# The first layer's modulation vectors summed on TensorE in column strips instead of on three other engines

## The chip, the cores and the metric

The kernel runs on one core of one Trainium2 chip. A core has TensorE (PE; its weight loads are shown as PEld), VectorE (DVE), ScalarE (ACT), GpSimd (POOL), SyncE (SP, whose queue issues nearly all transfers) and 16 DMA engines. The metric is the device time of one execution in microseconds. A time of the kernel is the median of several executions; the profile is one further execution with its own time.

## The reference

Two blocks run one after the other on a sequence of 256 rows and 1024 features, all in fp32. The first block has two layers. Each layer begins with a modulation vector of 6 x 1024 numbers (shift, scale and gate for the mixer, the same three for the feed-forward), made from one conditioning vector:

```python
c_act = jax.nn.silu(c)                       # [1, 1024]
for l in range(DEPTH):                       # DEPTH = 2
    mod = c_act @ w_mod[l] + b_mod[l]        # [1, 6144]
    shift1, scale1, gate1, shift2, scale2, gate2 = split(mod, 6)
    h = rms_norm(x, norm1) * (1.0 + scale1) + shift1
    proj = h @ w_in                          # pooled part, q, keys and values, gates
    ...                                      # pooling mixer, sparse attention
    x = x + gate1 * (mix @ w_out)
    h2 = rms_norm(x, norm2) * (1.0 + scale2) + shift2
    x = x + gate2 * (square(relu(h2 @ w_ff1)) @ w_ff2)
```

The second block (a state-space branch, a dilated attention, a feed-forward) has no modulation. What matters here is `c_act @ w_mod[l]`: a vector of 1024 times a matrix of 1024 x 1024 for each of the six parts.

## The kernel before

Large products run on TensorE as three products of rounded fp32 halves (high and low). Every weight tile of 128 x 1024 lands in one of five staging slots (`wst`); ScalarE makes the high half and VectorE the low one (`wh` L139, `wl` L140), and then the slot is free. Matrix products accumulate in four PSUM banks (`acc`); two banks (`st`), one (`tr`) and one (`pv`) serve everything else: scores, transposes, small products.

A modulation part is a sum over 1024 rows of the matrix, each scaled by one activation. The kernel keeps the activations as a tile `cact` of 128 x 8, so a tile of 128 matrix rows is scaled by one column of it. There are two routines. `first_mod(c)` (L603 to L617) makes, for 256 features of shift and scale, eight scaled sums of 128 x 512: VectorE adds the even ones (L611, L614), ScalarE scales the odd ones (L612, L615) and GpSimd adds them (L616). `first_norm` then sums over the partitions with eight products with a matrix of ones (`tr<-cst,acc`), makes the columns `mcol` (L627, L629), scales the transposed normed input (L638) and splits it into `hh` and `hl`. This is done in four parts, one for each quarter of the features; the products of q and k for part c, 24 on TensorE, follow it in `start()`. The four parts are staggered: the sums of part c+1 are written behind the q weight of part c.

`mod_part(l, q, eng)` (L536 to L580) makes a whole part of 1024 numbers in steps, one 512 KB tile a step. With `eng` 3, as for the first layer's parts 2, 3 and 4 (the mixer's gate, the feed-forward's shift and scale), five of eight tiles are added by VectorE (L547), three are scaled by ScalarE (L549) and added by GpSimd (L550) into `macc`. A gate is then split (L558, L559) and summed over the partitions into all rows (`mgate`); a shift or scale becomes a column (`mcol`). The steps are not placed by hand: each load of a weight tile takes as many of them as `rate` says.

```python
            self.due += self.rate
            while self.due >= 1.0 and self.extra:
                self.due -= 1.0
                self.step()
```

The rate is 0 at first and becomes `r0b` = 2 at step 14 of the first layer's plan. Gates are asked for by the residual after the output projection, shift and scale of the feed-forward just behind it. Five wide buffers of 128 x 1024 (`t4`) hold `macc` and `mgate`. The attention's steps are placed among the products by a plan with due times; within these bounds a scheduler fixes each engine's order ahead of time.

Of the kernel before, what the change touches and what calls it, by code (L numbers as in the profile page):

```python
# [16 lines left out]
D = 1024  # L17
# [7 lines left out]
ALPHA = 2.0 ** 0.25  # L25

SZ = 1024
TU = dict(nst=5, tabc=2, nw=9, nt2=22, raw=1, krest=2, qrest=4, pool2=1, c2=3, c3=1, c4=1, ln=3, uv='uv', pre=[1], nv=5, nv1=0, nv0=0, u0=19.5, du=0.7, ub=2, uc=4, c0=32.5, dc=0.1, w0=36, dw=0.5, comp=22, pool=27, dpool=2, cmpa=32, cmpb=34, dcmp=2, e1=1, e0=1, pta=2, ahead=3, modp=3, rf=0.95, r0=0, r0b=2, r1=0.8, r1b=1.2, rs=14, raw_=4, qrest_=6, u0_=19.5, du_=1.0, comp_=22, pool_=26, cmpa_=31, cmpb_=35, nv_=0, nv0_=0, w0_=32, dw_=0.8, order2='v0 qk0 qk1 qk2 v1 B C x0 x1 z0 x2 z1 x3 z2 z3 g2 g3 pa g0 g1 ps', dts=8, dcd=30, par0=10, par1=40, d0=50, dd=2, db=3, dc2=5, ss0=73, ds=4.2, scb=5, sx=3, sr=6, sg=3.5, sy=3.5, sn=8, sf=300, mf0=5, modp1=99, rf1=0.5, pool2_=3, c3_=2, c4_=3, nv1_=2, dpool_=2, dcmp_=1, dc_=0.4, cap=4, ub_=2.5, c0_=32.5, pta_=4)
NST, NW = TU['nst'], TU['nw']
NT2, NT4, NS5 = TU['nt2'], 5, 20  # L30

# [30 lines left out]
def tile_two_blocks(ctx: ExitStack, tc: tile.TileContext, I, out, stop=None, dbg=None):  # L62
# [451 lines left out]
    V.reciprocal(cact, cact)  # L514
    V.tensor_tensor(cact, cact, csrc, op=OP.mult)

    parc = [small.tile([128, NPS], FT, name=f"parc{l}", bufs=1) for l in range(DEPTH)]
    par = {}

# [17 lines left out]
    def mod_part(l, q, eng):  # L537
# [14 lines left out]
        if q in (2, 5):  # L552
            gt = t4([128, D], "mgate")
            parts = []
            for n in range(2):
                ns = slice(n * 512, (n + 1) * 512)
                ah, al = t2([128, 512], "mah", FR), t2([128, 512], "mal", FR)
                A.activation(ah, acc[:, ns], AF.Copy)  # L558
                G.tensor_tensor(al, acc[:, ns], ah, op=OP.subtract)  # L559
                parts.append((ah, al))  # L560
            for _ in range(3):
                yield
            for n, (ah, al) in enumerate(parts):
                b = bank("tr")
                mm(b, ones_r, al, True)
                mm(b, ones_r, ah, False, True)
                A.activation(gt[:, n * 512:(n + 1) * 512], b, AF.Copy)
            MC[l, q] = gt
        else:
            for _ in range(2):  # L570
                yield
            b = bank("tr")
            for j in range(8):
                mm(b[:, j * 64:(j + 1) * 64], acc[:, j * 128:(j + 1) * 128], ones[:, 0:64], j == 0, True)
            c = small.tile([128, 8], FT, name="mcol", bufs=6)
            i = {0: 0, 1: 1, 3: 2, 4: 3}[q]
            V.tensor_tensor(c, b.rearrange("p (j n) -> p j n", j=8)[:, :, 0], PS(l, "bmod")[:, i * 8:i * 8 + 8], op=OP.add)
            if q in (1, 4):
                V.scalar_tensor_tensor(c, c, 1.0, PS(l, "norm1" if q == 1 else "norm2"), op0=OP.add, op1=OP.mult)
            MC[l, q] = c  # L580

    ones_r = cp.tile([128, 128], FR, name="ones_r")

# [16 lines left out]
        xn = rms(t)  # L600
        later(TU["ln"], lambda: to_fm(t, xn, hi, lo, MC[l, q0 + 1], MC[l, q0]))

    def first_mod(c):  # L603

        acc = [t2([128, 512], "acc0") for _ in range(2)]
        for j in range(4):
            st = wp.tile([128, SZ], FT, name="wst", bufs=NST)
            nc.sync.dma_start(st, I["w_mod0"][c, j])
            sv, k = [st[:, i * 512:(i + 1) * 512] for i in range(2)], 2 * j
            if j == 0:  # L610
                V.tensor_scalar(acc[0], sv[0], cact[:, k:k + 1], None, op0=OP.mult)  # L611
                A.activation(acc[1], sv[1], AF.Copy, scale=cact[:, k + 1:k + 2])  # L612
            else:
                V.scalar_tensor_tensor(acc[0], sv[0], cact[:, k:k + 1], acc[0], op0=OP.mult, op1=OP.add)  # L614
                A.activation(sv[1], sv[1], AF.Copy, scale=cact[:, k + 1:k + 2])  # L615
                G.tensor_tensor(acc[1], acc[1], sv[1], op=OP.add)  # L616
        return acc  # L617

    def first_norm(xn, acc, hi, lo, c):
# [5 lines left out]
        m = small.tile([128, 4], FT, name="mcol0", bufs=2)  # L625
        bm = PS(0, "bmod")[:, 0:16].rearrange("p (q k) -> p q k", q=2)
        V.tensor_tensor(m.rearrange("p (q k) -> p q k", q=2), b[:, :256].rearrange("p (q k n) -> p q k n", q=2, k=2)[:, :, :, 0],  # L627
                        bm[:, :, 2 * c:2 * c + 2], op=OP.add)
        V.scalar_tensor_tensor(m[:, 2:4], m[:, 2:4], 1.0, PS(0, "norm1")[:, 2 * c:2 * c + 2], op0=OP.add, op1=OP.mult)  # L629
        b = bank("pv")  # L630
        for k in range(2):
            f = 256 * c + 128 * k
            for t in range(2):
                T.transpose(b[:, k * 256 + t * 128:k * 256 + t * 128 + 128], xn[t][f // 512][:, f % 512:f % 512 + 128], ident)
        hf = t2([128, 512], "hf")
        for k in range(2):
            ks = slice(k * 256, (k + 1) * 256)
            V.tensor_scalar(hf[:, ks], b[:, ks], m[:, 2 + k:3 + k], m[:, k:k + 1], op0=OP.mult, op1=OP.add)  # L638
        split(fl(hi[:, 2 * c:2 * c + 2]), fl(lo[:, 2 * c:2 * c + 2]), hf, A)

    def hybrid_layer(l, hilo, between, done):
# [1104 lines left out]
```

## Time and profile before

| what | value |
|---|---|
| time, median of 3 runs | 1291.28 us (1290.51 to 1297.46) |
| profiled execution, time | 1291.87 us |
| profiled execution, span from first to last instruction | 1290.1 us |
| TensorE busy | 1191.4 us, 92% |
| VectorE busy | 905.7 us, 70% |
| ScalarE busy | 640.3 us, 50% |
| GpSimd busy | 294.7 us, 23% |
| granted TensorE clock, mean | 0.973 |

Busy time is the time in which an engine ran an instruction. A busy TensorE need not be at its peak: its products are pipelined, and each row's duration has some drain in it that the next product overlaps. The first layer's q and k are made in about the first 65 us, its attention and output projection until about 180, its feed-forward until about 372.

### The profile page before, as it was taken

What the parts mean: (1) busy time and instruction counts of PE and PEld (TensorE: products, weight loads), DVE (VectorE), ACT (ScalarE), POOL (GpSimd) and SP (SyncE); (2) the same over time, 40 slices, a digit from 0 to 9 for tenths busy, and PEclk for the clock granted to TensorE, in tenths of its full rate; (3) what the DMA queues carried; (4) which work ended last, traced back from release to release, by engine and by line L of the source; (5) the groups of instructions that cost most, each with busy time, mean ns of one, the idle gap of its engine ahead of it and who ended that gap; (6) DMA issues with size and microseconds to landing.
All of it is one profiled execution on the core that took longest, in us unless ns stands there. A gap on an engine that the chain in (4) does not pass through costs nothing.

```text
span 1290.1 us, 19186 instructions
## 1 busy us (share of the span) xinstructions
PE 1191.4 (92%) x7242; PEld 1047.4 (81%) x7242; DVE 905.7 (70%) x1384; ACT 640.3 (50%) x1068; POOL 294.7 (23%) x281
## 2 busy tenths in 40 slices
PE   4868898999988999999999999998989999999997
PEld 3656776898977788799998999787688998789896
DVE  5877898877858768754446467899997557754544
ACT  4436355435436555645444355665674434554540
POOL 3543313103224101201010001434553001210101
PEclk9888989999999999999999999989998999999999
DMA  7855767998867525665654455244354643666640
GB/s 267 304 158 174 242 197 242 313 328 292 310 208 248 172 83 165 196 211 179 195 173 150 156 174 166 66 131 119 111 181 131 196 147 99 215 214 191 183 144 33
DMA packets 97028, 240.73 MB, mean 187 GB/s; under 512 B 9252, under 2 KB 14372, under 8 KB 96936
## 3 DMA queue, kind: packets, MB, share of 16 engines
q1 hardware_dynamic: 96296, 238.73, 57.8%
q8 instruction: 57, 0.93, 0.3%
q10 hardware_dynamic: 640, 0.79, 0.2%
q14 instruction: 35, 0.29, 0.1%
HBM read 237.65 MB, written 1.05 MB: 185 GB/s over the span
## 4 chain that ended last, share of the span: by engine, by line
PE 38%; issue 10%; DVE 9%; ACT 1%; POOL 1%; DMA 0%; DVEq 0%; ACTq 0%; POOLq 0%
PE acc L88 23%; PE st L88 12%; DVE wl L140 3%; DVE G L1420 2%; DVE E L1431 1%; PE pv L88 1%; DVE cv L1315 1%; ACT wh L139 1%; DMA wst<-in_w_up_dram 0%; POOL yss L118 0%; DVE yg L1462 0%; DVE ytmp L1450 0%; DVE yg L1457 0%; POOL fr L379 0%; PE tr L88 0%
## 5 line engine op out<-in xcount | busy, mean ns | idle before, releaser
L140 DVE TENSOR_TENSOR wl<-wst,wh 128x1024 fp32r<-128x1024 f32 (+3 forms) x340 | 427.3, 1269 | 173.0 <-ACT wh L139 171.4
L139 ACT ACTIVATE wh<-wst 128x1024 fp32r<-128x1024 f32 (+3 forms) x340 | 351.7, 1048 | 311.3 <-PE acc L88 113.6
L88 PE MATMUL st<-hh,wh 128*128 128x256 f32 x576 | 163.0, 283 | 0.0
L88 PE MATMUL st<-hl,wh 128*128 128x256 f32 x576 | 163.0, 283 | 0.0
L88 PE MATMUL st<-hh,wl 128*128 128x256 f32 x576 | 163.0, 283 | 0.0
L88 PE MATMUL acc<-wh,frl 128*128 128x512 f32 x384 | 151.2, 394 | 2.3 <-DVE frl L380 2.1
L379 POOL TENSOR_TENSOR fr<-fr 128x512 f32<-128x512 f32 x48 | 63.5, 1323 | 382.4 <-ACT frh L378 376.0
L88 PE MATMUL acc<-wl,frh 128*128 128x512 f32 x384 | 149.8, 390 | 0.0
L88 PE MATMUL acc<-wh,frh 128*128 128x512 f32 x384 | 149.7, 390 | 0.0
L88 PE MATMUL acc<-hh,wl 128*128 128x256 f32 x416 | 122.5, 295 | 2.3 <-DVE wl L140 2.3
L88 PE MATMUL acc<-hl,wh 128*128 128x256 f32 x416 | 119.9, 288 | 0.0
L88 PE MATMUL acc<-hh,wh 128*128 128x256 f32 x416 | 119.8, 288 | 0.0
L88 PEld LDWEIGHTS st<-hl,wh 128*128 128x128 f32 x576 | 110.5, 192 | 0.7
L88 PEld LDWEIGHTS st<-hh,wl 128*128 128x128 f32 x576 | 110.5, 192 | 0.7
L88 PEld LDWEIGHTS st<-hh,wh 128*128 128x128 f32 x576 | 110.5, 192 | 0.0
L88 PE MATMUL acc<-wl,hh 128*128 128x512 f32 (+3 forms) x224 | 89.7, 401 | 15.2 <-DVE wl L140 15.2
L547 DVE SCALAR_TENSOR_TENSOR macc<-wst,cact,macc 128x1024 f32<-128x1024 f32 x70 | 92.3, 1318 | 7.0 <-DMA wst<-in_w_mod_dram 4.5
L88 PE MATMUL acc<-wh,hl 128*128 128x512 f32 (+3 forms) x224 | 88.3, 404 | 3.3 <-DVE hl L105 2.7
L88 PE MATMUL acc<-wh,hh 128*128 128x512 f32 (+3 forms) x224 | 90.2, 403 | 0.0
L88 PEld LDWEIGHTS acc<-wh,frl 128*128 128x128 f32 x384 | 72.1, 188 | 19.3 <-DVE frl L380 5.4
L88 PEld LDWEIGHTS acc<-hh,wl 128*128 128x128 f32 x416 | 81.6, 196 | 4.7 <-DVE wl L140 3.1
L88 PEld LDWEIGHTS acc<-wh,frh 128*128 128x128 f32 x384 | 72.1, 188 | 15.3
(326 smaller groups left out, 2365.6 us busy)
## 6 DMA issues: line engine op xcount, KB each, us to landing
wst<-in_w_ff_dram SPq DMA_DIRECT2D x128, 512.0 KB, 4.4
wst<-in_w_mod_dram SPq DMA_DIRECT2D x96, 512.0 KB, 4.5
wst<-in_w_in_dram SPq DMA_DIRECT2D x92, 512.0 KB, 4.7
wst<-in_w_up_dram SPq DMA_DIRECT2D x32, 512.0 KB, 4.5
wst<-in_w_down_dram SPq DMA_DIRECT2D x32, 512.0 KB, 4.4
wst<-in_w_out_dram SPq DMA_DIRECT2D x24, 512.0 KB, 4.5
wst<-in_w_proj_ssd_dram SPq DMA_DIRECT2D x16, 512.0 KB, 3.6
wst<-in_w_in_dram SPq DMA_DIRECT2D x8, 384.0 KB, 3.8
```

What stands on the lines that cost most here:

```text
L88: T.matmul(o, l, r, start=start, stop=stop, skip_group_check=True)
L139: A.activation(h[:, :kc * n], st[:, :kc * n], AF.Copy)
L140: V.tensor_tensor(l[:, :kc * n], st[:, :kc * n], h[:, :kc * n], op=OP.subtract)
L379: G.tensor_tensor(r, r, r, op=OP.mult)
L547: V.scalar_tensor_tensor(acc, st, cact[:, k:k + 1], acc, op0=OP.mult, op1=OP.add)
L1315: V.scalar_tensor_tensor(v[:, a:e], u[:, a + j - 2:e + j - 2], w[:, j:j + 1], v[:, a:e], op0=OP.mult, op1=OP.add)
L1420: V.scalar_tensor_tensor(gm[:, i], cl, dt_[:, t, 32 + a0 + i:33 + a0 + i], gm[:, i], op0=OP.mult, op1=OP.add)
L1431: V.tensor_tensor(E, E, ssd.pop(("G", g, t, sub)), op=OP.mult)
```

## The change

All of `first_mod` and, for the first layer's parts 2, 3 and 4, `mod_part` give way to sums on TensorE. The activations are copied into a tile `cb` in which each of the eight columns stands 32 times. A product with 32 such columns as its weights gives 32 equal rows of sums in 32 of the 128 output partitions. The eight products of a group go to four strips of 32 columns by turns, two to each strip, so that the bank holds four partial sums, each 32 times. ScalarE copies the bank out. A product with a selector (`sel`, one row of each strip) adds the four and turns the row into columns; for the gate the selector stands in all 128 columns (`sel_all`), with the gate's bias added as row 1.

In the start, parts 0 and 1 are summed ahead of the first column sums, and part c+2 behind the k products of part c. The new `mod_sums` takes two tiles of 128 x 4 x 256 a step from the wide buffers, no longer from the weights' staging slots, and has five steps in place of ten or eleven. The rate `r0b` goes from 2 to 1.2. The remaining parts (those of the second layer, and the first layer's last gate) stay with `mod_part`.

```diff
+    cb = cp.tile([128, 8, 32], FT, name="cb")
+    V.tensor_copy(cb, cact[:, :, None].to_broadcast([128, 8, 32]))
+    sel = cp.tile([128, 2], FT, name="sel")
+    sel_all = cp.tile([128, 128], FT, name="sel_all")
...
+    def mod_sums(l, q):
+        acc = t4([128, D], "mrow")
+        def load(i):
+            ts = [t4([128, 4, 256], "mst") for _ in range(2)]
+            for j in range(2):
+                c = q * D + i * 256
+                nc.sync.dma_start(ts[j], I["w_mod"][l, j * 512:(j + 1) * 512, c:c + 256].rearrange("(k p) n -> p k n", p=128))
+            return ts
+        ts = load(0)
+        for i in range(4):
+            yield
+            b = bank("tr")
+            for k in range(8):
+                r = slice((k % 4) * 32, (k % 4) * 32 + 32)
+                mm(b[r, :256], cb[:, k], ts[k // 4][:, k % 4], k < 4, k >= 4)
+            A.activation(acc[:, i * 256:(i + 1) * 256], b[:, :256], AF.Copy)
+            if i < 3:
+                ts = load(i + 1)
+        if q in (2, 5):
+            nc.sync.dma_start(acc[1:2, :], I["b_mod"][l:l + 1, q * D:(q + 1) * D])
+            gt = t4([128, D], "mgate")
+            yield
+            for n in range(2):
+                ns = slice(n * 512, (n + 1) * 512)
+                b = bank("tr")
+                mm(b, sel_all, acc[:, ns], True, True)
+                A.activation(gt[:, ns], b, AF.Copy)
+            MC[l, q] = gt
+        else:
+            yield
+            b = bank("tr")
+            for j in range(8):
+                mm(b[:, 2 * j:2 * j + 2], acc[:, j * 128:(j + 1) * 128], sel, j == 0, True)
+            mod_columns(l, q, b[:, :16].rearrange("p (j n) -> p j n", j=8)[:, :, 0])
...
-    def first_mod(c):
-        acc = [t2([128, 512], "acc0") for _ in range(2)]
+    def first_rows(c):
+        b = bank("st")
         for j in range(4):
             st = wp.tile([128, SZ], FT, name="wst", bufs=NST)
             nc.sync.dma_start(st, I["w_mod0"][c, j])
-            sv, k = [st[:, i * 512:(i + 1) * 512] for i in range(2)], 2 * j
-            if j == 0:
-                V.tensor_scalar(acc[0], sv[0], cact[:, k:k + 1], None, op0=OP.mult)
-                A.activation(acc[1], sv[1], AF.Copy, scale=cact[:, k + 1:k + 2])
-            else:
-                V.scalar_tensor_tensor(acc[0], sv[0], cact[:, k:k + 1], acc[0], op0=OP.mult, op1=OP.add)
-                A.activation(sv[1], sv[1], AF.Copy, scale=cact[:, k + 1:k + 2])
-                G.tensor_tensor(acc[1], acc[1], sv[1], op=OP.add)
-        return acc
+            for i in range(2):
+                k = 2 * j + i
+                r = slice((k % 4) * 32, (k % 4) * 32 + 32)
+                mm(b[r], cb[:, k], st[:, i * 512:(i + 1) * 512], k < 4, k >= 4)
+        rows = t2([128, 512], "rows0")
+        A.activation(rows, b, AF.Copy)
+        return rows
...
-        for i in range(2):
-            for j in range(4):
-                mm(b[:, j * 64:(j + 1) * 64], acc[i][:, j * 128:(j + 1) * 128], ones[:, 0:64], i == 0 and j == 0, i == 1)
+        for j in range(4):
+            mm(b[:, 2 * j:2 * j + 2], rows[:, j * 128:(j + 1) * 128], sel, j == 0, True)
...
             accs = {n: [bank("acc") for _ in range(2)] for n in "qk"}
-            acc = first_mod(0)
-            first_norm(xn0, acc, hi, lo, 0)
+            rows = [first_rows(0), first_rows(1)]
+            first_norm(xn0, rows[0], hi, lo, 0)
             for c in range(4):
                 for n in "qk":
                     wh, wl = W.next()
-                    if n == "q" and c < 3:
-                        acc = first_mod(c + 1)
...
                     if n == "q" and c < 3:
-                        first_norm(xn0, acc, hi, lo, c + 1)
+                        first_norm(xn0, rows[c + 1], hi, lo, c + 1)
+                    if n == "k" and c < 2:
+                        rows.append(first_rows(c + 2))
...
+    for i in range(2):
+        V.reduce_sum(sel[:, i:i + 1], ident[:, 0:128:32], axis=AX.X)
+    V.tensor_tensor(sel_all, sel[:, 0:1].to_broadcast([128, 128]), ident[:, 1:2].to_broadcast([128, 128]), op=OP.add)
...
-    W.extra.extend(mod_part(*m, TU["modp"]) for m in MODS["mix", 0])
+    W.extra.extend(mod_sums(*m) for m in MODS["mix", 0])
```

## Rows read from the trace of the kernel before

**Rows 1.** The page's busy time, share of the span and instructions of each engine.
```profile
PE 1191.4 (92%) x7242; PEld 1047.4 (81%) x7242; DVE 905.7 (70%) x1384; ACT 640.3 (50%) x1068; POOL 294.7 (23%) x281
```
**Rows 2.** Busy time by stretch: us, engines with instructions, granted clock, DMA share, GB/s.
```profile
21.90:62.20 40.30, 33.53 (x142) 25.52 (x143) 32.16 (x38) 17.21 (x24) 20.29 (x21) 0.92 0.83 286
62.20:97.00 34.80, 24.27 (x110) 19.67 (x109) 25.86 (x57) 12.77 (x21) 17.07 (x31) 0.85 0.54 174
97.00:137.00 40.00, 29.70 (x176) 23.53 (x175) 28.83 (x72) 24.91 (x56) 14.52 (x14) 0.91 0.59 197
137.00:180.00 43.00, 42.15 (x265) 36.13 (x263) 38.90 (x91) 20.30 (x53) 13.06 (x6) 0.96 0.69 226
...
220.00:372.00 152.00, 149.31 (x953) 135.13 (x952) 116.08 (x105) 73.08 (x87) 35.49 (x29) 1.00 0.87 297
```
**Rows 3.** Waits of TensorE from 62 to 180: us in total, times, longest.
```profile
PE acc L88 <- DVE wl L140: 10.1, 3, 6.7
PE tr L88 <- DVE chv L836: 4.3, 1, 4.3
PE acc L88 <- DVE ml L105: 2.9, 1, 2.9
```
**Rows 4.** Groups by line, 0 to 62: count, busy us, mean ns, idle before.
```profile
L616 POOL TENSOR_TENSOR acc<-acc,wst 128x512 f32<-128x512 f32 x12 | 18.6, 1551 | 23.1 <-ACT wst L615 16.6 <-ACT acc L612 6.0
L614 DVE SCALAR_TENSOR_TENSOR acc<-wst,cact,acc 128x512 f32<-128x512 f32 x12 | 15.3, 1275 | 0.4
```
**Rows 5.** Groups by line, 62 to 180.
```profile
L550 POOL TENSOR_TENSOR macc<-macc,wst 128x1024 f32<-128x1024 f32 x9 | 21.3, 2369 | 42.5 <-DVE macc L547 26.4 <-ACT wst L549 16.1
L547 DVE SCALAR_TENSOR_TENSOR macc<-wst,cact,macc 128x1024 f32<-128x1024 f32 x15 | 19.1, 1275 | 2.2 <-POOL macc L550 2.2
```
**Rows 6.** Order of time in the start: start us, duration us, instruction, idle before.
```profile
8.89 0.72 ACT L612 ACTIVATE acc<-wst,cact 128x512 f32<-128x512 f32 x1
...
12.69 0.72 ACT L615 ACTIVATE wst<-wst,cact 128x512 f32<-128x512 f32 x1 [0.57 <-DMA wst<-in_w_mod_dram]
...
15.04 3.67 PE L88 MATMUL tr<-cst,acc 128*128 128x64 f32 x16 [3.50 <-DVE acc L614]
...
21.93 0.80 PE L88 MATMUL acc<-wh,hl 128*128 128x512 f32 x1 [0.56 <-DVE hl L105]
...
24.03 8.66 SPq L608 DMA_DIRECT2D wst<-in_w_mod_dram  x4
...
65.12 0.58 ACT L716 ACTIVATE kS<-acc 128x512 f32<-128x512 f32 x1
```
**Rows 7.** Order of time, single products on TensorE at several places.
```profile
22.53 0.63 PE L88 MATMUL acc<-wl,hh 128*128 128x512 f32 x1
...
97.51 1.13 PE L88 MATMUL st<-kT,qT 64*128 64x256 f32 x8
...
157.21 0.39 PE L88 MATMUL acc<-wh,ml 128*128 128x512 f32 x1
157.44 1.02 PE L88 MATMUL tr<-vbd,pcT 128*128 128x512 f32 x2
```
**Rows 8.** Order of time, places around waits from 55 to 136.
```profile
55.48 1.42 POOL L659 TENSOR_TENSOR tab<-par,cst 128x32 f32<-128x32 f32 x2 [3.93 <-DMA par<-in_par_dram]
...
68.12 1.66 POOL L118 TENSOR_TENSOR hr<-hss,half 128x8 f32<-128x8 f32 x1
...
81.49 2.37 POOL L550 TENSOR_TENSOR macc<-macc,wst 128x1024 f32<-128x1024 f32 x1
81.55 2.46 DVE L681 TENSOR_TENSOR sq<-sq,hr 128x128 f32<-128x128 f32 x1 [0.90 <-POOL hr L118]
...
113.81 1.18 DVE L678 TENSOR_TENSOR ckr<-ckr,csq 32x64 f32<-32x64 f32 x1
...
132.96 1.28 DVE L547 SCALAR_TENSOR_TENSOR macc<-wst,cact,macc 128x1024 f32<-128x1024 f32 x1 [0.71 <-POOL macc L550]
...
135.10 1.15 ACT L549 ACTIVATE wst<-wst,cact 128x1024 f32<-128x1024 f32 x1 [3.05 <-DMA wst<-in_w_mod_dram]
```

More of the change, by code (lines that the diff above doesn't have):

```diff
@@ L27 @@
 SZ = 1024
-TU = dict(nst=5, tabc=2, nw=9, nt2=22, raw=1, krest=2, qrest=4, pool2=1, c2=3, c3=1, c4=1, ln=3, uv='uv', pre=[1], nv=5, nv1=0, nv0=0, u0=19.5, du=0.7, ub=2, uc=4, c0=32.5, dc=0.1, w0=36, dw=0.5, comp=22, pool=27, dpool=2, cmpa=32, cmpb=34, dcmp=2, e1=1, e0=1, pta=2, ahead=3, modp=3, rf=0.95, r0=0, r0b=2, r1=0.8, r1b=1.2, rs=14, raw_=4, qrest_=6, u0_=19.5, du_=1.0, comp_=22, pool_=26, cmpa_=31, cmpb_=35, nv_=0, nv0_=0, w0_=32, dw_=0.8, order2='v0 qk0 qk1 qk2 v1 B C x0 x1 z0 x2 z1 x3 z2 z3 g2 g3 pa g0 g1 ps', dts=8, dcd=30, par0=10, par1=40, d0=50, dd=2, db=3, dc2=5, ss0=73, ds=4.2, scb=5, sx=3, sr=6, sg=3.5, sy=3.5, sn=8, sf=300, mf0=5, modp1=99, rf1=0.5, pool2_=3, c3_=2, c4_=3, nv1_=2, dpool_=2, dcmp_=1, dc_=0.4, cap=4, ub_=2.5, c0_=32.5, pta_=4)
+TU = dict(nst=5, tabc=2, nw=9, nt2=22, raw=1, krest=2, qrest=4, pool2=1, c2=3, c3=1, c4=1, ln=3, uv='uv', pre=[1], nv=5, nv1=0, nv0=0, u0=19.5, du=0.7, ub=2, uc=4, c0=32.5, dc=0.1, w0=36, dw=0.5, comp=22, pool=27, dpool=2, cmpa=32, cmpb=34, dcmp=2, e1=1, e0=1, pta=2, ahead=3, modp=3, rf=0.95, r0=0, r0b=1.2, r1=0.8, r1b=1.2, rs=14, raw_=4, qrest_=6, u0_=19.5, du_=1.0, comp_=22, pool_=26, cmpa_=31, cmpb_=35, nv_=0, nv0_=0, w0_=32, dw_=0.8, order2='v0 qk0 qk1 qk2 v1 B C x0 x1 z0 x2 z1 x3 z2 z3 g2 g3 pa g0 g1 ps', dts=8, dcd=30, par0=10, par1=40, d0=50, dd=2, db=3, dc2=5, ss0=73, ds=4.2, scb=5, sx=3, sr=6, sg=3.5, sy=3.5, sn=8, sf=300, mf0=5, modp1=99, rf1=0.5, pool2_=3, c3_=2, c4_=3, nv1_=2, dpool_=2, dcmp_=1, dc_=0.4, cap=4, ub_=2.5, c0_=32.5, pta_=4)
 NST, NW = TU['nst'], TU['nw']
@@ L574, in mod_part @@
                 mm(b[:, j * 64:(j + 1) * 64], acc[:, j * 128:(j + 1) * 128], ones[:, 0:64], j == 0, True)
[L575 to L580, printed above, removed]
+            mod_columns(l, q, b.rearrange("p (j n) -> p j n", j=8)[:, :, 0])
@@ L582, in tile_two_blocks, with mod_columns @@
+    def mod_columns(l, q, src):
+        c = small.tile([128, 8], FT, name="mcol", bufs=6)
+        i = {0: 0, 1: 1, 3: 2, 4: 3}[q]
+        V.tensor_tensor(c, src, PS(l, "bmod")[:, i * 8:i * 8 + 8], op=OP.add)
+        if q in (1, 4):
+            V.scalar_tensor_tensor(c, c, 1.0, PS(l, "norm1" if q == 1 else "norm2"), op0=OP.add, op1=OP.mult)
+        MC[l, q] = c
     ones_r = cp.tile([128, 128], FR, name="ones_r")
@@ L608, in first_mod, with first_norm @@
             nc.sync.dma_start(st, I["w_mod0"][c, j])
-            sv, k = [st[:, i * 512:(i + 1) * 512] for i in range(2)], 2 * j
-            if j == 0:
-                V.tensor_scalar(acc[0], sv[0], cact[:, k:k + 1], None, op0=OP.mult)
-                A.activation(acc[1], sv[1], AF.Copy, scale=cact[:, k + 1:k + 2])
-            else:
-                V.scalar_tensor_tensor(acc[0], sv[0], cact[:, k:k + 1], acc[0], op0=OP.mult, op1=OP.add)
-                A.activation(sv[1], sv[1], AF.Copy, scale=cact[:, k + 1:k + 2])
-                G.tensor_tensor(acc[1], acc[1], sv[1], op=OP.add)
-        return acc
-    def first_norm(xn, acc, hi, lo, c):
-        b = bank("tr")
-        for i in range(2):
-            for j in range(4):
-                mm(b[:, j * 64:(j + 1) * 64], acc[i][:, j * 128:(j + 1) * 128], ones[:, 0:64], i == 0 and j == 0, i == 1)
[L625 to L630, printed above, removed]
+            for i in range(2):
[5 more added lines that the diff above has]
+        return rows
+    def first_norm(xn, rows, hi, lo, c):
+        b = bank("tr")
+        for j in range(4):
+            mm(b[:, 2 * j:2 * j + 2], rows[:, j * 128:(j + 1) * 128], sel, j == 0, True)
+        bt = bank("pv")
         for k in range(2):
@@ L633, in first_norm @@
             for t in range(2):
-                T.transpose(b[:, k * 256 + t * 128:k * 256 + t * 128 + 128], xn[t][f // 512][:, f % 512:f % 512 + 128], ident)
+                T.transpose(bt[:, k * 256 + t * 128:k * 256 + t * 128 + 128], xn[t][f // 512][:, f % 512:f % 512 + 128], ident)
+        m = small.tile([128, 4], FT, name="mcol0", bufs=2)
+        bm = PS(0, "bmod")[:, 0:16].rearrange("p (q k) -> p q k", q=2)
+        V.tensor_tensor(m.rearrange("p (q k) -> p q k", q=2), b[:, :8].rearrange("p (q k n) -> p q k n", q=2, k=2)[:, :, :, 0],
+                        bm[:, :, 2 * c:2 * c + 2], op=OP.add)
+        V.scalar_tensor_tensor(m[:, 2:4], m[:, 2:4], 1.0, PS(0, "norm1")[:, 2 * c:2 * c + 2], op0=OP.add, op1=OP.mult)
         hf = t2([128, 512], "hf")
@@ L637, in first_norm @@
             ks = slice(k * 256, (k + 1) * 256)
-            V.tensor_scalar(hf[:, ks], b[:, ks], m[:, 2 + k:3 + k], m[:, k:k + 1], op0=OP.mult, op1=OP.add)
+            V.tensor_scalar(hf[:, ks], bt[:, ks], m[:, 2 + k:3 + k], m[:, k:k + 1], op0=OP.mult, op1=OP.add)
         split(fl(hi[:, 2 * c:2 * c + 2]), fl(lo[:, 2 * c:2 * c + 2]), hf, A)
```

## The prediction

> **What bounds the kernel now.** I read the page's busy shares first, then the busy time by stretch, then who TensorE waited for, then the order of time in the first 180 us, the only part that the change touches. TensorE is busy 92% of the span [rows 1], but the shares differ by stretch [rows 2]: 33.5 of 40.3 us in most of the first layer's q and k (21.9 to 62.2), 24.3 of 34.8 in the next stretch, 29.7 of 40 in the one after, 42.2 of 43 from 137 to 180, and 149.3 of 152 in the feed-forward. So the feed-forward follows TensorE alone, and what is won or lost ahead of it reaches the end nearly whole. A microsecond taken from another engine is worth something only where TensorE waits.
>
> In the start the turn from part to part sets the pace: sums on three engines, column sums on TensorE, normed tile, 24 products, next part. The first product starts at 21.93, and the first copy out of the finished k at 65.12 [rows 6]: 43 us for four parts, of which 96 products at 0.23 us [rows 7] are 22. VectorE's 12 long sums take 15.3 us, GpSimd's 12 adds 18.6 [rows 4]. They hold the staging slots: four issues of modulation tiles take the queue from 24.03 to 32.69 [rows 6].
>
> From 62 to 180 TensorE waits in three places above all [rows 3]: 10.1 us for split weights (one wait of 6.7), 4.3 in the compression, 2.9 for a split of the pool branch. In rows 8 one sees a part of this caused by the modulation sums: a GpSimd add runs from 81.49 to 83.86, and a small VectorE product that started beside it takes 2.46 us; another small one takes 1.18 at 113.81; a sum of 1.28 stands ahead of a split at 132.96. After each wait TensorE works at its lower clock for a while: the granted clock is 0.85, 0.91 and 0.96 in the three stretches [rows 2], and a product of 512 columns, 0.39 us long at 2.4 GHz, takes 0.63 at 1.2 GHz [rows 7].
>
> **What the new sums cost.** An fp32 product is two passes: the two in 1.02 us with 512 columns [rows 7] are 0.43 each and 0.17 of drain. Rows 7 also have four products of 256 columns on two row strips, eight passes in 1.13 us; in a line they would take 8 x 0.213 = 1.70 and the drain, so the strips ran at the same time. No row shows column strips side by side. The bounds are full overlap, as on the row strips, and none, as in the pair of 512. I take full overlap, nearest to the row of two strips. A group of eight products of 512 columns then costs 4 x 0.43 = 1.7 us, 1.9 with edges; of 256 columns 0.85, 1.05 with edges. In a line they would be 6.9 and 3.4.
> The Trainium skill (TensorE: Matmul & The Clock Gate, Part 3, Measured speedup vs the span model) gives 2.38 times for three column tiles, not 3. By that factor the groups would be about 2.9 and 1.45 us by estimate; no row here can say, and a rival below takes a partial overlap of its own.
>
> **Start.** Removed are the 15.3 us on VectorE, 18.6 on GpSimd and 16 ScalarE scalings; 16 column-sum passes a part become 8. The 16 took 3.67 us at the lower clock [rows 6], so 8 are 0.9 at the higher one. Added are four groups of eight, one ScalarE copy each, and an order: two parts are now summed ahead of the first column sums. The first four tiles came from 8.89 to 12.69, 1.27 us apart [rows 6]; the next four need the slots that TensorE frees after them, so they are here by 18 and summed by 19. From the end of the column sums (15.04 + 3.67) to the first product (21.93) it was 3.2 us; with 0.9 for the sums, part 0 begins at 23, 1 us later than now. From there TensorE does 5.5 us of products a part, 1.4 of column sums and transposes for the next, and 1.9 of sums for the one after, the last in parts 0 and 1 alone: 8.8 + 8.8 + 6.9 + 5.5 = 30 us. In part 2 the q weight gets a slot only once part 1's weights are split and comes 2.4 us late, 2.4 + 30 = 32.4. The last k product is done at 55.5 to 56, against 65. But the next stretch does not start with k alone: the rotation tables on GpSimd wait for their inputs until 55.48, and the power operation behind them that VectorE needs starts at 68.12 [rows 8]; the wait of 6.7 us hangs on it. Those inputs queue behind the slots too: part 3's sums are done at 23 + 17.6 = 40.6, and with five tiles' worth of transfers at 1.27 they land at about 48, 7.5 sooner. I take the smaller: **-7.5**. If part 0 runs at the lower clock, its 12 products of q cost 12 x 0.24 = 2.9, and if the inputs land two tiles later another 2.5; if part 0's column sums go ahead of part 1's late tiles, 1.5 more. So -2.1 to -9. The strip copies of the activations and the selector (three or four small VectorE operations) fall before the input is there, while VectorE is idle; uncovered they cost under 1 us once.
>
> **62 to 180.** Removed: 15 sums (19.1 us) on VectorE, 9 adds (21.3) on GpSimd [rows 5], 9 scalings on ScalarE. I count only what shortens a wait of TensorE. The 2.46 us product becomes about 0.3: 2.2 of a wait. In the compression chain the small product (1.18) and the power operation no longer stand beside or behind the gate's split on GpSimd: 3 of the 4.3. The sum at 132.96 and its like: 2 of 2.9. A weight split slowed by a GpSimd add: 1. The clock not granted in the three stretches is 0.15 x 34.8 + 0.09 x 40 + 0.04 x 43 = 10.5 us, waits included [rows 2]; where three waits go I take 4.4 of it back. Together 12.6. Four passes of the gate's split go: 4 x 0.213 = 0.85. In the wait of 6.7 us, which I leave standing (the GpSimd chain above), two groups of sums can hide: 2.1. Gains 15.5.
> Added: three parts of four groups, 12 x 1.05 = 12.6, and the gate row by two fp32 products, 1.7: 14.3. Column sums of the other two parts stay 16 passes each. The new ScalarE copies are shorter than the scalings they replace. Net **-1.2**; with no wait shortened but the hidden groups it is +11, with the 6.7 gone too -8.
>
> The rate edit (2 to 1.2 steps a weight load) stretches 15 steps over 12.5 loads where 31 took 15.5; a step loads two tiles, so the modulation bytes come a little sooner. They leave the weights' staging slots for the five wide buffers, and their issues stand on the same SyncE queue as the weights. Costed at nothing, since the queue carries 174 to 226 GB/s there and 286 in the start [rows 2].
>
> **Sum.** 1291.87 (the profiled execution, span 1290.1 and 1.8 around it) - 7.5 - 1.2 = 1283.2. The median of the runs is 0.6 lower, which I don't carry.
>
> **Rivals.**
> *Strips in a line.* For it: no row shows column strips together. Against it: the two row strips. The start loses 4.9 in each of parts 2 and 3 and some 5 ahead of part 0, 15 together; 12 groups of 3.4 in place of 0.85 add 31, of which some 4 hide in waits. 1283 + 15 + 27 = 1325, slower.
> *Partial overlap*, half way in speed between the two strips of the row and four: groups of 6.9 / 3 = 2.3 and 1.15 us plus edges. The start gives back about 2, the 12 groups 4, and 1 to 2 us of cover go: near 1290.5, no change. The factor of the Trainium skill named above speaks for this case.
> *A wait in place of the one removed.* The three parts use the one bank that transposes, compression and attention share, and ScalarE must copy it out. ScalarE waits in order: at 135.10 it had stood 3.05 us for a landing [rows 8]. A copy queued behind a weight's split keeps the bank, and TensorE's next transpose waits. With 12 copies, 1.15 us each (14 us) gives 1297, and 1.3 each is 0.5% slower; from 0.7 each on the gain is gone. With the gate row alive only three of the five wide buffers are left for tiles, so a load can hold the queue until TensorE comes to its group; the queue's order then delays the next weight in the same way. Against it: most copies can go when ScalarE is between landings.
> *More than counted.* The wait of 6.7 us hangs on GpSimd, whose tables can start when their inputs land; they could land sooner than I have it, up to all of the wait. 1283 - 6.5 = 1276.5.
>
> **How the numbers follow.** My case 0.50, 1274 to 1294 by its bounds; line 0.12; partial 0.14; new wait 0.15; more 0.09. A measurement tells 0.5%, 6.5 us, from no change, so faster means under 1284.8 and slower over 1297.7. My case lies near that edge: 0.32 faster, 0.17 same, 0.01 slower. Partial 0.03, 0.09, 0.02; new wait 0.07 same, 0.08 slower; line 0.12 slower; more 0.09 faster. Faster 0.44, same 0.33, slower 0.23. The range 1274 to 1306 leaves out the line case and the tails, under 0.2.
>
> **What the profile would show.** Right: the 256-column passes of four strips starting within some 10 ns and a group of eight done in about 1 us; part 0's first product near 23 and the last k product near 56; no VectorE product of 2.4 us near the k rotation; TensorE's wait in the compression under 2 us. Wrong: passes one after another at 0.21 us; new TensorE waits on a ScalarE copy of the summed rows; SyncE issues of the new tiles that take several us with weights late behind them; a lower granted clock in the start.

## The result, and the profile after

The changed kernel takes 1304.72 us (median of 4 runs, 1302.77 to 1306.85); the kernel before took 1291.88 beside it (1290.51 to 1297.46). The ratio is 1.0094, with a 95% interval from 1.0065 to 1.0122: slower by about 12 us, where 8 to 9 us faster was forecast. The profiled execution took 1302.77, its span is 1300.9.

Busy time by stretch after the change (us, then each engine with its instructions, granted clock, DMA share, GB/s):

```profile
21.90:62.20 40.30, 35.59 (x159) 24.03 (x158) 16.78 (x28) 13.53 (x18) 11.89 (x35) 0.87 0.91 318
62.20:97.00 34.80, 29.70 (x184) 22.00 (x182) 25.69 (x75) 19.03 (x41) 6.54 (x5) 0.95 0.70 215
97.00:137.00 40.00, 32.52 (x208) 22.47 (x206) 17.59 (x48) 18.15 (x43) 5.45 (x6) 0.91 0.62 202
137.00:180.00 43.00, 36.37 (x267) 26.73 (x269) 20.25 (x75) 13.04 (x44) 1.29 (x1) 0.95 0.43 133
```

Beside [rows 2]: VectorE (the third pair) is relieved in three of the four, from 38.9 to 20.3 us in the last. TensorE (the first) is busier in the first three, as intended. But from 137 to 180, where it had been busy for 42.2 of 43 us, it now stands for 6.6, and the transfers fall from 226 to 133 GB/s. What it waits for from 62 to 192, beside [rows 3]:

```profile
PE acc L88 <- DVE wl L140: 4.7, 1, 4.7
PE tr L88 <- DMA mst<-in_w_mod_dram: 4.5, 2, 3.8
PE tr L88 <- DVE chv L881: 2.9, 1, 2.9
PE tr L88 <- DVE ml L105: 1.5, 1, 1.5
```

Of the three waits that the change aimed at, two are shorter (10.1 to 4.7 us and 4.3 to 2.9), and the third, ahead of the output projection, is gone. The 1.5 for `ml` is another one: inside the projection a group waits for the shared bank, which VectorE's split still reads. 4.5 us of a new wait, for the summed tiles themselves (`mst`), have come. In order of time, TensorE's groups of sums at some places, and one product of the gate row (two passes):

```profile
32.98 1.92 PE L88 MATMUL st<-wst,cb 128*32 128x512 f32 x16
...
118.31 2.08 PE L88 MATMUL tr<-mrow,sel_all 128*128 128x512 f32 x2 [0.32 <-DVE vc L888]
...
134.38 1.07 PE L88 MATMUL tr<-mst,cb 128*32 128x256 f32 x16
...
157.25 1.07 PE L88 MATMUL tr<-mst,cb 128*32 128x256 f32 x16
...
174.05 0.64 PE L88 MATMUL tr<-mst,cb 128*32 128x256 f32 x8 [3.76 <-DMA mst<-in_w_mod_dram]
175.46 1.00 PE L88 MATMUL tr<-mst,cb 128*32 128x256 f32 x8 [0.77 <-DMA mst<-in_w_mod_dram]
...
179.60 1.93 PE L88 MATMUL tr<-mst,cb 128*32 128x256 f32 x16 [1.47 <-DVE ml L105]
...
188.65 0.64 PE L88 MATMUL tr<-mst,cb 128*32 128x256 f32 x8
```

Sixteen passes in 1.07 us (256 columns) and 1.92 (512) are the full overlap of four strips. From 157 on, though, the groups follow their tiles, which land one by one: the last six take from 157.25 to 189.29, and the group at 179.60, behind a pause, takes 1.93 for the work that took 1.07, at the lower of the two clock levels (granted 0.50 from 179.6 to 181.4). The cause of the late tiles stands in SyncE's queue (waits from 62 to 200, and the issue itself):

```profile
SPq L591 <- PE tr L88: 44.8, 9, 21.9
```
```profile
135.08 25.23 SPq L591 DMA_DIRECT2D mst<-in_w_mod_dram  x5
```

Of the 25 us of these five issues, 21.9 are one wait: the third needs a wide buffer that TensorE gives back with its group at 157.25. Between the group at 134.38 and that one TensorE's order, fixed ahead of time, has attention and output projection.

Where the time went is seen by cutting the first layer at three instructions: `hr`, the power operation behind the tables; the first product of the output projection; and `rtmp`, the first gated row of the residual. Before they stand at 68.1, 136.4 and 176.7 us, after at 63.6, 133.5 and 190.3. The stretches between them, before and then after:

```profile
68.10:136.40 68.30, 47.46 (x256) 37.89 (x254) 51.32 (x122) 31.74 (x68) 25.77 (x22) 0.88 0.53 168
...
136.40:176.70 40.30, 39.45 (x244) 33.67 (x245) 36.20 (x87) 19.91 (x52) 13.06 (x6) 0.96 0.68 222
```
```profile
63.60:133.50 69.90, 57.33 (x352) 40.92 (x351) 41.88 (x119) 34.11 (x75) 11.96 (x11) 0.93 0.67 213
...
133.50:190.30 56.80, 50.17 (x354) 35.62 (x355) 22.22 (x77) 16.57 (x53) 3.51 (x3) 0.91 0.46 140
```

4.5 us are won ahead of `hr`, 1.6 lost in the first stretch, 16.5 in the second: 13.6 at `rtmp`. Of the 16.5, 10.7 are TensorE's busy time and 5.8 its idle time (0.85 to 6.63). Of the 13.6, 10.8 are left at the end of the span.

### The profile page after: what moved, and what is told of

The parts are those of the page before. It is cut to its first block, busy times and chain, and to the rows that moved or that the text cites. A ratio compares the mean times of both kernels' runs of the same rounds, so it can differ in the third digit from the quotient of the medians.

```text
span 1300.9 us, 19520 instructions
## 1 busy us (share of the span) xinstructions
PE 1214.4 (93%) x7466; PEld 1044.6 (80%) x7466; DVE 857.5 (66%) x1357; ACT 625.2 (48%) x1057; POOL 250.7 (19%) x255
## 3 DMA queue, kind: packets, MB, share of 16 engines
HBM read 237.65 MB, written 1.05 MB: 183 GB/s over the span
## 4 chain that ended last, share of the span: by engine, by line
PE 37%; issue 10%; DVE 9%; DMA 1%; ACT 1%; POOL 1%; DVEq 0%; ACTq 0%; POOLq 0%
PE acc L88 22%; PE st L88 12%; DVE wl L140 3%; DVE G L1468 2%; DMA wst<-in_w_in_dram 1%; DVE E L1479 1%; PE pv L88 1%; DVE cv L1363 1%; ACT wh L139 1%; DMA wst<-in_w_down_dram 0%; POOL yss L118 0%; DVE yg L1510 0%; DVE yg L1505 0%; POOL fr L379 0%; PE st L1318 0%
## 5 line engine op out<-in xcount | busy, mean ns | idle before, releaser
L140 DVE TENSOR_TENSOR wl<-wst,wh 128x1024 fp32r<-128x1024 f32 (+3 forms) x340 | 423.0, 1258 | 187.4 <-ACT wh L139 185.9
L88 PEld LDWEIGHTS acc<-wl,frh 128*128 128x128 f32 x384 | 73.0, 190 | 14.2
```

What stands on the lines that cost most here:

```text
L88: T.matmul(o, l, r, start=start, stop=stop, skip_group_check=True)
L140: V.tensor_tensor(l[:, :kc * n], st[:, :kc * n], h[:, :kc * n], op=OP.subtract)
```

## The experiments

The theory after this reading: the loss is in the mixer's sums, and it is tiles that land late because their wide buffers are freed late by TensorE. The first rival: TensorE's added passes are the loss wherever the tiles lie. The second: the start, whose gain fell short. Ratios are to the kernel before, run beside each on the same chip.

**The two halves.** The start alone (the mixer's parts as before, rate 2):
```diff
-    W.extra.extend(mod_sums(*m) for m in MODS["mix", 0])
+    W.extra.extend(mod_part(*m, TU["modp"]) for m in MODS["mix", 0])
```


> The changed start alone; the mixer's three parts are again summed by VectorE, ScalarE and GpSimd, at the rate of before. Theory (the loss sits in the mixer's groups and their five wide buffers; the start's gain is small because part 0's ScalarE copy stands behind the copy of part 1's rows): the key ends about 1 us earlier, the rope tables 6 us earlier, the first operation on the rope tables' user hr 4 to 5 us earlier, and 2 to 6 us of that reach the end: 1286 to 1290 us. Rival (my prediction's own step, the start is worth 7.5 us): 1284 or less. Rival (the start is itself slower): over 1292.


Measured 1286.62, ratio 0.9963 (0.9945 to 0.9982): the start gains 5 us, and the rest of the change costs 17. Three rows of it in order of time:
```profile
24.14 0.47 PE L88 MATMUL acc<-wh,hl 128*128 128x512 f32 x1 [1.33 <-DVE hl L105]
...
46.63 0.24 POOL L704 TENSOR_TENSOR tab<-par,cst 128x32 f32<-128x32 f32 x1 [37.00 <-DMA par<-in_par_dram]
...
61.57 0.58 ACT L761 ACTIVATE kS<-acc 128x512 f32<-128x512 f32 x1
```
The tables' input is there 8.9 us sooner than in [rows 8]; the first copy out of the key begins only 3.6 sooner than in [rows 6]. In the 14 profiles that have this start and five slots it begins at 61.1 to 65.0, so one profile alone says little about a microsecond or two here.

The sums of the mixer alone (`first_mod` and `first_norm` of before put back):

> The start of before, and only the mixer's three parts summed by TensorE, at the changed rate. Theory: the whole loss is here, with the residual's first gated row some 13 to 17 us later than before: 1303 to 1309 us, as slow as the full change or slower. Rival (the two parts of the change harm each other, as when the changed start shifts the loads): within 5 us of before, 1288 to 1297.


Measured 1307.95, ratio 1.0127 (1.0101 to 1.0152); `rtmp` at 193.8. As the theory had it; the start is not the loss.

**The rate edit** undone in the full change (`r0b=2`).

> The full change with the rate edit alone undone (2 in place of 1.2). Theory (SyncE's queue waits for wide buffers that TensorE frees): the groups are asked for earlier, the same buffers run short, and part of the pile of groups ahead of the output projection goes: 1298 to 1304. Rival (the rate edit is what makes the last groups late): 1285 to 1294. Rival (TensorE's added work is the loss wherever it stands): within 2 us of the full change, 1303 to 1307.


Measured 1313.12, ratio 1.0158 (1.0135 to 1.0181). None of the three: slower. The groups come earlier, and the output projection begins 13 us later (146.4), but `rtmp` at 191.7 is only 1.4 us behind the full change; the other 10 us of the two profiles come after it. From `rtmp` to 240 TensorE is busy for 37.4 of 48.3 us, and for 45.3 of 49.7 in the full change; why is open. The lower rate is a gain of some 8 us of this kernel, not its fault.

**Passes or loads.** Three kernels. The tiles loaded once a part, for its first group alone; half of the products left out; and the 18 loads put back into two tiles that nothing reads (with nineteen small buffers in place of 22):
```diff
-            if i < 3:
-                ts = load(i + 1)
```
```diff
-            for k in range(8):
+            for k in range(4):
...
-                mm(b[r, :256], cb[:, k], ts[k // 4][:, k % 4], k < 4, k >= 4)
+                mm(b[r, :256], cb[:, k], ts[k % 2][:, k], True, True)
```
```diff
-            ts = [t4([128, 4, 256], "mst") for _ in range(2)]
+            ts = [t4([128, 4, 256], "mst") if not i else wp.tile([128, 4, 256], FT, name="unread", bufs=2) for _ in range(2)]
...
-                ts = load(i + 1)
+                load(i + 1)
```


> The full change, but each part loads its weights for the first of its four column groups only, and the other three groups sum the same two tiles again: 18 of the 24 loads are left out (three quarters of each part's sums are of the wrong columns), every pass of TensorE stays. Theory (the late loads and the queue behind them are most of the loss; seven wide buffers gave back 4 to 5 us): no wait for a modulation tile is left, the residual's first gated row comes within 3 us of its time before, 1285 to 1293 us. Rival (TensorE's added passes are the loss): 1297 to 1303.

> The full change with all its loads, but each group of eight products cut to four, one in each strip (half of each sum is left out). Twelve groups fall from about 1.05 to 0.55 us. Theory (loads and the queue): 1300 to 1305 us, within 4 us of the full change. Rival (TensorE's added passes are the loss): at least their 6 us come back, with what they push, 1292 to 1298.

> The run that loaded a quarter of the tiles, with the other 18 loads back in SyncE's queue at their places, but into two tiles of their own that no product reads (three quarters of each part's sums are of the wrong columns, as there; nineteen small buffers to make room). All bytes move again and nothing waits for TensorE's groups to free them. Theory (what costs is the wait for free buffers and for the tiles that then land late): 1287 to 1294 us, as without those loads (1290.4). Rival (the bytes themselves, or 24 more issues in the queue, delay the weights): 1298 to 1305.


Measured 1290.39, ratio 0.9982 (0.9966 to 0.9998); 1305.51, ratio 1.0097 (1.0076 to 1.0118); 1289.04, ratio 0.9973 (0.9955 to 0.9992). With all passes and few loads the loss is gone; with half the passes and all loads it is all there; with all passes and all bytes, but no buffer to wait for, it is gone too. So it is the groups' wait for tiles that themselves wait for buffers, neither the passes nor the bytes. The stretch up to `rtmp` in the first, and its queue's wait from 56 to 200:
```profile
130.20:175.70 45.50, 45.46 (x352) 34.14 (x353) 24.27 (x78) 15.28 (x52) 4.45 (x3) 1.00 0.14 43
```
```profile
SPq L591 <- PE tr L88: 42.6, 2, 35.9
```
TensorE does not stop once, at the full clock. With all its passes this stretch takes 5.2 us more than the 40.3 of before, and 11.3 less than the 56.8 of the change. Of these 11.3, 6.6 were idle time, and by an estimate from the granted clock (0.09 x 56.8) 5.1 were the clock. SyncE waits for TensorE nearly as long as in the change (44.8, in the same window), and nothing is lost: here the queue's wait alone costs nothing, since no tile comes late by it.

**More wide buffers, or another queue.** Seven in place of five, with three small buffers fewer; the control with the small ones alone; and the tiles' loads on GpSimd's queue (`nc.gpsimd.dma_start`):
```diff
-NT2, NT4, NS5 = TU['nt2'], 5, 20
+NT2, NT4, NS5 = 19, 7, 20
```


> The full change with seven wide buffers in place of five (19 small ones in place of 22, to make room). Theory: with five free tiles the load of a group no longer waits for TensorE to finish the group before it; SyncE's 45 us of waits for TensorE fall below 15 us, the groups from 157 us on find their tiles there, and 6 to 14 us come back: 1290 to 1299. Rival (TensorE's added work is the loss): within 3 us of the full change, 1302 to 1308. Three small buffers fewer may cost some of it.

> The full change with nineteen small buffers in place of 22 and five wide ones: the control of the run with seven wide buffers, whose profile was 8.4 us ahead of the full change at the residual's first gated row and 5.4 us at the end. Theory (the three small buffers cost 3 to 4 us, in the last block, and the two wide ones alone are worth 8): 1306 to 1310 us, the loss between the end of the second layer and the end. Rival (the small buffers cost nothing): 1302 to 1306.

> The full change with the 24 loads of the mixer's groups issued by GpSimd's queue in place of SyncE's, so that the waits for wide buffers hold no weight behind them; GpSimd's own work of that stretch stands behind them instead. Theory (the queue is what is lost): SyncE's waits for TensorE's groups disappear and 4 to 10 us come back, 1295 to 1300 us. Rival (the late tiles themselves and TensorE's work are the loss, not what stands behind them in the queue): within 3 us of the full change, 1302 to 1308. Rival (GpSimd's work comes late instead): over 1308.


Measured 1300.52, ratio 1.0069 (1.0047 to 1.0091); 1304.16, ratio 1.0098 (1.0068 to 1.0128); 1311.79, ratio 1.0146 (1.0122 to 1.0169). Two more buffers take TensorE's wait for the tiles from 4.5 to 0.6 us, yet SyncE still waits 40.4 us for TensorE, not under 15 as expected. In the runs a quarter of the loss comes back, short of the theory's range, and the two intervals overlap, so that even this is not clear of noise. In its profile the second stretch is mended (48.3 us against 56.8), the first is not (69.7 against 69.9):
```profile
63.90:133.60 69.70, 56.80 (x351) 40.42 (x349) 41.83 (x119) 33.97 (x75) 12.07 (x11) 0.93 0.71 229
...
133.60:181.90 48.30, 46.28 (x354) 34.06 (x355) 22.07 (x77) 16.70 (x53) 4.50 (x3) 1.00 0.44 142
```
The small buffers cost nothing that the runs can tell. On GpSimd's queue the wait is moved, not removed: GpSimd stands 51.0 us for TensorE's groups, and TensorE 5.8 for tiles.

**Another ring.** The tiles in the weights' staging ring (`wst`), five deep as it is, nothing else changed; then that ring eight deep, with four wide buffers and nineteen small ones; then this ring for the kernel before, and for the start alone:
```diff
-            ts = [t4([128, 4, 256], "mst") for _ in range(2)]
+            ts = [wp.tile([128, SZ], FT, name="wst", bufs=NST).rearrange("p (k n) -> p k n", k=4) for _ in range(2)]
```
```diff
-TU = dict(nst=5, ...
+TU = dict(nst=8, ...
...
-NT2, NT4, NS5 = TU['nt2'], 5, 20
+NT2, NT4, NS5 = 19, 4, 20
```


> The full change with its tiles in the weights' staging ring as it is, five deep, no buffer added or taken anywhere. Theory (the number of buffers is what counts): tiles and weights share five, the queue waits for TensorE as before, 1298 to 1310 us. Rival (the wide buffers, with the rows and the gate among them, were the trouble, not the number): 1286 to 1295.

> The full change, all its loads read, with the tiles in the ring of the weights' staging buffers, made eight deep, in place of the wide buffers (four of those, nineteen small ones, to make room). Theory (the shortage of buffers is what costs): fewer us of wait for TensorE on SyncE's queue than the 45 of the full change, and 1293 to 1300 us. Rival (tiles that wait for TensorE's turn now hold the weights' own buffers): over 1302.

> The kernel before with the staging ring eight deep, four wide buffers and nineteen small ones, and nothing of the change: the control of the run at 1282.0 us. Theory (the ring is short only where TensorE reads the tiles in its own order; VectorE, ScalarE and GpSimd gave theirs back quickly): 1287 to 1294 us. Rival (a deeper ring is worth the whole difference by itself): 1279 to 1285.

> The changed start alone with the same ring of eight, the mixer's parts summed as before. In the run at 1282.0 us the key ended 8.9 us earlier than before and the first operation on the tables' user 12.3 us earlier, where five staging buffers gave 1 to 4 and 5 to 7. Theory (the start's tiles, held until TensorE comes to them, want the deeper ring; the mixer's sums are then worth nothing either way): 1278 to 1284 us, the same as 1282.0 within 3 us. Rival (the mixer's sums gain by themselves): 1285 to 1290.


Measured, in this order: 1293.89, ratio 1.0000 (0.9982 to 1.0017); 1282.01, ratio 0.9915 (0.9890 to 0.9939); 1295.56, ratio 1.0016 (1.0000 to 1.0032); 1289.20, ratio 0.9976 (0.9956 to 0.9996). The first is the rival's: no buffer is added, the tiles only change rings, and the whole loss is gone. So it was not the number of buffers in all that was short, as my theory had it: the loss sat in the wide ring, with the row and a live gate in two of its five. That the three left were simply too few is not shown, since seven leave five and gave back a quarter at most. With the rings the queue's order changes too: here, from 62 us on, one to four tiles at a time are issued between the weights, up to 163 us, in the change six in a row from 82.6 and ten from 116.8. The scheduler orders every engine anew in each kernel, and no run holds that order fixed.

The second is faster than both kernels, and faster than its theory had it. The deeper ring gives nothing to the kernel before, and no more to the start alone than it had without it; with it the mixer's sums gain by themselves, 8 us over the start with the same ring (from `hr` to `rtmp` 112.6 us against 124.4, of which TensorE is idle for 9.8 and 27.4). A part of the 8 us is the control's own loss. With this ring and four wide buffers that stretch is longer where the other engines do the sums: 117.6 us in place of 108.6 in the kernel before, 124.4 in place of 110.2 in the start alone (two profiles that lie 5 us above and 4 below the medians of their runs). Over the start alone with five slots, ring and sums together gain 6 us. The waits of the queue and the same stretches, five deep and then eight deep:
```profile
SPq L591 <- PE tr L88: 22.6, 9, 10.9
```
```profile
60.90:126.80 65.90, 55.46 (x368) 40.11 (x366) 36.69 (x114) 30.02 (x71) 9.60 (x11) 0.97 0.50 160
...
126.80:175.40 48.60, 46.97 (x342) 34.31 (x339) 21.89 (x77) 16.28 (x53) 3.46 (x3) 0.96 0.61 192
```
```profile
SPq L591 <- PE tr L88: 26.5, 7, 16.6
```
```profile
55.80:124.00 68.20, 58.40 (x369) 42.47 (x367) 38.62 (x116) 32.02 (x73) 11.36 (x11) 0.91 0.62 196
...
124.00:168.40 44.40, 44.40 (x339) 34.18 (x336) 22.25 (x78) 17.75 (x54) 3.46 (x3) 0.98 0.53 176
```
The queue still waits for TensorE, about half as long; TensorE no longer waits for a tile. With eight the start moves as well, in order of time:
```profile
39.52 1.92 PE L88 MATMUL st<-wst,cb 128*32 128x512 f32 x16
...
56.24 0.58 ACT L761 ACTIVATE kS<-acc 128x512 f32<-128x512 f32 x1
```
Part 3's sums run in one piece, where in the change they stand in three from 39.55 to 46.49; their loads are issued from 24.24 here and from 34.54 there. The first copy out of the key begins 8.9 us sooner than before; in the start alone with this ring it begins at 59.44, 5.7 sooner.

**The order in the start.** The start alone, with part 0's norm ahead of part 1's rows:
```diff
-            rows = [first_rows(0), first_rows(1)]
+            rows = [first_rows(0)]
             first_norm(xn0, rows[0], hi, lo, 0)
+            rows.append(first_rows(1))
```


> The changed start alone, as in the first run, but with the norm of part 0 put before the products of part 1's rows, so that ScalarE's rounding of the first activation no longer stands behind the copy of part 1's rows. Theory: the first product of the query comes 1 to 2 us earlier than 24.1, and 0 to 2 us of it reach the end: 1284 to 1287. Rival (the products wait for the weights, not for the activation): the same time as the first run, 1286 to 1288.


Measured 1288.03, ratio 0.9964 (0.9947 to 0.9982), as the start alone. The activation was ready earlier (`hh` at 18.9 in place of 21.1), but the rounding of the first weight, on ScalarE, still stood behind the copy of part 1's rows and began at 22.05; the first product came at 25.0.

**Without strips.** The mixer's groups in one strip, one product after another (`mm(b[:32, :256], cb[:, k], ..., k == 0, k == 7)`).

> The full change, with the twelve groups of the mixer's parts kept in one strip of 32 columns, one product after another (the start keeps its four strips); the sums are the same. A pass of 256 columns takes 0.216 us where sets of four start every 0.216 us now, so a group of eight products (16 passes) should take 3.4 to 3.5 us in place of 1.05, and twelve groups 29 us more of TensorE. Theory (the eight groups from 133 us on stand on a full TensorE, those before in its idle time): 15 to 25 us on the full change, 1320 to 1330. Rival (the tiles are what TensorE waits for, so longer groups hide in the waits): 1306 to 1314.


Measured 1321.17, ratio 1.0228 (1.0188 to 1.0267): 17 us on the full change.
```profile
144.03 3.64 PE L88 MATMUL tr<-mst,cb 128*32 128x256 f32 x16
```

**Parts one by one**, with the start, tiles in the wide buffers: the gate alone by TensorE at rate 2, the gate alone at 1.65, the other two parts alone at 1.5.

> The changed start, and of the mixer's three parts only the first, the gate, summed by TensorE; the other two by VectorE, ScalarE and GpSimd, at the rate of before. Its four groups fall between 70 and 110 us, where TensorE has idle time. Theory (late loads cost in the full stretch from 137 us on; groups that TensorE takes in its idle time cost little): 1282 to 1289 us, as fast as the start alone (1286.6) or some us faster. Rival (a group costs its time wherever it stands, and its tiles hold the queue): 1290 to 1295.

> The run with only the gate summed by TensorE, at a rate of 1.65 in place of 2. There the gate took fewer steps, so the other two parts came to VectorE sooner, and VectorE was as busy from 61 to 139 us as without the change (50.9 us against 53.2): the added work of TensorE came on top of the same idle time (18 us). Theory (VectorE's relief is what pays for TensorE's groups, and the pace gave it away): the idle time falls by 3 to 6 us, 1287 to 1293 us. Rival (the groups and the gate cost their time whatever VectorE does): 1294 to 1298.

> The changed start, the gate summed as before, and the other two parts, whose groups fall late, by TensorE, at a rate of 1.5. Theory: nearly the whole loss of the mixer's sums (18 us between the full change and the start alone) is here: 1298 to 1306 us. Rival (the loss goes by the number of parts, a third for each): 1295 to 1299. Rival (it was the first part that pushed the rest late): under 1292.


Measured 1296.42, ratio 1.0033 (1.0014 to 1.0052); 1305.96, ratio 1.0106 (1.0072 to 1.0140); 1309.96, ratio 1.0151 (1.0117 to 1.0185). Against the start alone (0.9963) that is 9, 18 and 24 us more: the parts don't add up to the 17 of all three, and none of the theory's ranges held. From `hr` to the output projection, the start alone, then the gate at rate 2, then at 1.65:
```profile
61.10:130.40 69.30, 50.96 (x272) 40.18 (x270) 53.16 (x124) 35.22 (x74) 25.78 (x21) 0.87 0.54 174
```
```profile
60.70:139.10 78.40, 60.32 (x337) 43.95 (x335) 50.94 (x124) 38.29 (x82) 24.65 (x19) 0.84 0.63 209
```
```profile
63.00:148.00 85.00, 61.87 (x337) 44.78 (x335) 52.48 (x124) 36.77 (x77) 21.97 (x18) 0.80 0.57 181
```
TensorE's busy time grows by 9 to 11 us while its idle time stays at 18 us and then rises to 23: VectorE, still with two parts to sum, is no freer (51 to 53 us). That a lower rate would give the idle time back was wrong; why it rose is open. In these kernels the wide ring also holds the sums of the other parts (`macc`), and no run takes them out of it.

## Why the prediction was wrong, step by step

**The strips: right.** Groups of 1.07 and 1.92 us against 1.05 and 1.9. By the Trainium skill's factor of 2.38 for three strips (TensorE: Matmul & The Clock Gate, Part 3, Measured speedup vs the span model) a group of 256 columns was to take about 1.45 by estimate; against 3.64 in line, four strips here are 3.4 times as fast, so the trace does not bear out the slower case. The rival of strips in a line was off in its size too: 12 x 2.57 = 31 us more of TensorE cost 17 in time.

**The start: right about the tables, wrong about the key.** Forecast 7.5 us, limited by the tables' inputs: in the start alone they came 8.9 sooner, and 5 us (2.3 to 7.1 by the interval) were left at the end. The term that failed is the key at 55.5 to 56: 61.6 in the start alone, 64.0 in the change. Part 0's first product, forecast for 23, came at 24.1 and 25.8. And I had given the q weight of part 2 one delay of 2.4 us and let part 3's tiles land in time; their loads wait for the five slots (SyncE stands 18.8 us for the start's groups from 10 to 47 in the change). With eight slots the key stood at 56.24, and at 59.44 in the start alone.

**What was added: mis-sized.** Forecast 14.3 us, 0.85 of gate passes saved. From `hr` to `rtmp` the rows have 16.5 for the twelve groups and 4.1 for the gate row:
```profile
L88 PE MATMUL tr<-mst,cb 128*32 128x256 f32 x192 | 16.5, 426 | 6.7 <-DMA mst<-in_w_mod_dram 4.5 <-DVE ml L105 1.5 <-issue 0.7
...
L88 PE MATMUL tr<-mrow,sel_all 128*128 128x512 f32 x4 | 4.1, 1141 | 0.3 <-DVE vc L888 0.3
```
I priced every group in one piece and at the full clock. Five of the twelve stand in two pieces, 1.28 to 1.72 us together; three ran wholly or partly at half the clock; and each product of the gate took some 2.08 us where [rows 7] have 1.02 at the full clock.

**What was gained: there only when the tiles are.** I took 15.5 us from TensorE's waits and its clock. From `hr` to `rtmp`, by the rows above and the same view of the others (busy and idle time of TensorE, us):

| kernel | busy | idle | sum | ratio |
|---|---|---|---|---|
| before | 86.9 | 21.7 | 108.6 | 1 |
| the change | 107.5 | 19.2 | 126.7 | 1.0094 |
| seven wide buffers | 103.1 | 14.9 | 118.0 | 1.0069 |
| tiles in the ring of five | 102.4 | 12.1 | 114.5 | 1.0000 |
| tiles in the ring of eight | 102.8 | 9.8 | 112.6 | 0.9915 |
| loaded once | 104.3 | 9.5 | 113.8 | 0.9982 |

The sums put 15 to 21 us on TensorE in every row but the first. What pays for them is its idle time: 10 to 12 us of it go where the tiles are on time, 2.5 where they are late. Even then this stretch is 4 us longer than before, so -1.2 was too good by some 5; what the best kernel gains on the one before is all ahead of it, with `hr` 12 us sooner. My case's upper bound was also added up wrongly: its own terms, -2.1 and +11, make 1300.8 and not 1294, and the measured time lies behind that too.

**The step that failed** is "costed at nothing, since the queue carries 174 to 226 GB/s there": I moved the loads from a ring that other engines drain quickly into three buffers that only TensorE frees, in its own order, at the place where [rows 2] show it full (42.2 of 43 us), and looked at bandwidth in place of buffers. Its price is the step from 1.0094 to 1.0000, 12 us, at the same number of buffers in all. The rival of a new wait named this in its second half and came nearest (1297), but it had the weights late behind the tiles, and what came late were the tiles: from 130 to 191 TensorE waits 4.5 us for them and for no weight. Its first half, ScalarE's copy that holds the bank, is hardly seen: TensorE waits 0.6 and 0.5 us for it. **The rate edit**, costed at nothing too, was worth 8 us in the full change.

**Left open:** what it is in the wide ring that makes the tiles late; why seven wide buffers, five of them for tiles, leave the first stretch as long as it was, where the shared ring of five has it at 65.9; why single parts cost more than their share, and how the 13.6 us at `rtmp` shrink to 10.8 at the end, in work that the change doesn't touch.

## What to carry to other kernels

When sums move from engines with slack to the one that is full, their operands are freed in the full engine's order: count how many buffers its tiles can have next to what lives in the same ring, and how long the engine leaves the last one unread, before looking at bandwidth. A load that waits for a buffer at the head of a queue costs nothing while its tile still lands before its turn, so read the consumer's wait for the tile, not the queue's wait for the buffer. And try the other ring first: here that one line was worth the whole loss.

## What the runs showed of the hardware that I had not expected

Four column strips of 32 overlap fully in fp32: sixteen passes of 256 columns take 1.07 us in four strips and 3.64 in one. And a pause costs more than its length: the same sixteen passes took 1.93 us, at a granted clock of 0.50, behind waits of 3.76, 0.77, 0.57 and 1.47 us in the ten us before.

A queue's wait says little by itself: SyncE stood 44.8 us for TensorE in the kernel at 1.0094, and 42.6 in the one at 0.9982.
